# Homes of mLSTM row tiles, y operands and last-stage pools moved; loads and splits at three seams issued in order of use

## The chip, the core and the metric

The kernel runs on one core of one Trainium2 chip. The metric is device time in microseconds (us) of one execution; the figure for a kernel is the median of its runs. The changed kernel computes the same function with the same matrix products.

## The reference, cut to what matters

```python
# layer 0: mLSTM mixer (x: 2048 tokens x 1024), layer 1: RG-LRU mixer, then a final RMSNorm
u = rmsnorm(x, ln_g[0])
xm, z, o_pre, i_pre, f_pre = split(u @ w_in)                # 2048 wide each, gates 4 heads
xc = silu(causal_dwconv(xm, conv_w, conv_b))
q, k, v = xc @ w_q * DK**-0.5, xc @ w_k, xm @ w_v           # per head
h = mlstm_chunkwise(q, k, v, log_i, log_f)                  # C_new = d*C + sum w k v ; num/den
y = (norm(sigmoid(o_pre) * h) * norm_w + skip * xc) * silu(z)
x = x + y @ w_out
u = rmsnorm(x, ln_g[1])
xr, g = split(u @ r_w_in)                                   # 1536 wide each
xc = causal_dwconv(xr, ...)
r, ig = sigmoid(xc @ w_a + b_a), sigmoid(xc @ w_x + b_x)    # 8 diagonal blocks of 192
hs = linear_scan(exp(log_a), sqrt(-expm1(2*log_a)) * ig * xc)
x = x + (hs * silu(g)) @ r_w_out
out = rmsnorm(x, final_g)
```

## The kernel before, in words

Activations lie transposed, 128 channels by 512 (or 256) tokens. Every fp32 product is done as three fp32r matmuls: `split_into` makes a high part (`hi`, a cast on ScalarE, line 790) and a low part (`lo`, a subtraction on VectorE, line 793), and `mm3` (lines 390 to 392) multiplies hi by hi, and hi and lo crosswise. Weights come as fp32 (`raw`) and are split on the spot, or come back already split from a store in DRAM (`kept`). Names with `d_` are arrays in DRAM.

There are four stages.

- **a1**: the input projection, by a Strassen-like scheme of seven products of half-sized blocks, run by a `Slab` object. It stores xm, xc, z, o and the decay rows to DRAM.
- **a2**: the mLSTM, 4 heads by 8 blocks of 256 tokens. A block loads its `xm`, `xc`, `sz`, `o`, and two row tiles broadcast over the partitions, `qb` and `db` (function `rows`). GpSimd masks `qb`, ScalarE makes the weights `wgt` from it, VectorE multiplies the projected q by `db` (`qd`); then come k (`kT`, line 950), the scores (`s`, line 965), v from `vwh`/`vwl`, the state `C` and its split `Ch`/`Cl`, numerator `n`, and the result `hh` (line 1057), which is normalised (`frs`, on GpSimd) and stored as `d_y`.
- **b1**: the out-projection with the residual. `x1_slab(s)` runs once for each half of the tokens, again by seven products in the order u11, t2, u21, t3, t1, t4, u22. Its operands are quarters of y (`y_load`, quarters 11, 12, 21, 22, four tiles `t` each), or sums and differences of them (`into`, line 1225). `get_y` splits an operand ahead of its use, `stream` loads and splits a weight ahead of its use; both run at high priority. Behind them come the RMS sums (`ssum`, line 1142, and `stx`, line 1145, called by `stat`) and the input projection of layer 1 (`early`, `alternate`, groups), which stores `xr` and the gate `g`.
- **b2**: the gates of the RG-LRU (`gate`, from 768 KB weights `wg`), the scan, and the last projection (`acc`, from 512 KB weights `wr`). A block of 512 tokens has four parts p = 0 to 3 of three tiles each; a part's gates use two `wg` tiles, 18 matmuls each. `xch`/`xcl` are the split operand of a part, `yh`/`yl` the split result of one.

Each engine, and each DMA queue (SP's and GpSimd's), takes its instructions strictly in the order in which they were put. That order is made by a scheduler from the program's order, its priorities, and `order(first, then)`, which makes `then` follow `first` on the same engine. Tiles come from pools; a tile's place in SBUF is shared in time with earlier tiles, and the first write to it waits until the earlier tile's last reader is done.

In the kernel before, `y_load` puts all loads of y behind the last instruction of the last block's normalisation: `self.order(self.rooted, (d,))` (line 1213).

The pools of b2 are opened, on the left side of SBUF, in the order r4, y4, w4, x4, g4, t4 (`w4` holds `wr`, `g4` holds `wg`, `t4` holds `xc`, `x4` holds `xch`/`xcl`, `y4` holds `yh`/`yl`).

Of the kernel before, what the change touches and what calls it, by code (L numbers as in the profile page):

```python
# [14 lines left out]
P = 128  # L15
# [33 lines left out]
class Slab:  # L49


    def __init__(self, K, ctx, gain, paired=False, banks=None):
# [22 lines left out]
        self.places = {}  # L75
# [10 lines left out]
    def pair(self, nm, j, dtype=F32):  # L86

        return (self.ta if nm in ("t3", "u22") else self.tp).tile([P, 2 * TB], dtype, tag=f"{nm}{j}", name=f"{nm}{j}")
# [27 lines left out]
    def split(self, t, keep=None):  # L116

        w = t.shape[1]
        both = self.slot(w)
        hi, lo = both[:, 0:w], both[:, w:2 * w]  # L120
        self.K.split_into(hi, lo, t, "a", "v")
        if keep is not None:
            self.nc.gpsimd.dma_start(keep, both.bitcast(F32))
        return hi, lo
# [213 lines left out]
class Trunk:  # L338
# [465 lines left out]
    def phase_a2(self, wq, wk, wv, rgate, rwout, D, late):  # L804
# [3 lines left out]
        with ExitStack() as ctx:  # L808
# [69 lines left out]
            def project(h, b):  # L878
# [7 lines left out]
                def rows():  # L886
                    S["qb"] = qb = lp.tile([P, 2, P], F32, tag="qb", name="qb")
                    S["db"] = db = lp.tile([P, BL], F32, tag="db", name="db")
                    nc.sync.dma_start(qb, D["q"][r0:r0 + 2].rearrange("c t -> (c t)").partition_broadcast(P)
# [3 lines left out]
                def loads():  # L893
# [6 lines left out]
                    nc.sync.dma_start(xc, D["xc"][hs, :, bs].rearrange("k p t -> p k t"))  # L900
                    nc.sync.dma_start(xm, D["xm"][hs, :, bs].rearrange("k p t -> p k t"))
# [5 lines left out]
                    nc.sync.dma_start(sz, D["sz"][hs, :, bs].rearrange("k p t -> p k t"))  # L907
                    self.loaded = (nc.sync.dma_start(o, D["o"][b * 2:b * 2 + 2, :, h * DV:(h + 1) * DV].rearrange("c p n -> p c n")),)
                    for nm, x in (("xc", xc), ("xm", xm)):
# [9 lines left out]
                def qk():  # L919
# [3 lines left out]
                    wgt = dp.tile([P, 2, P], F32, tag="wgt", name="wgt")  # L923
                    for c in range(2):
                        a = nc.scalar.activation(wgt[:, c], qb[:, c], AF.Exp, bias=self.gT[:, r0 + c:r0 + c + 1],
                                                 scale=-1.0)
                        if (h, b) == (0, 1):
                            self.order((self.kT,), (a,))
                    S["wgt"] = wgt
                    xh, xl = S["xc"]  # L930
                    for nm in ("q", "k"):
# [6 lines left out]
                        t = dp.tile([P, 2, BL], F32, tag=nm + "T", name=nm + "T")  # L938
# [17 lines left out]
                    for k in range(KV):  # L956
                        nc.scalar.activation(skx[:, k], S["xcf"][:, k], AF.Copy, scale=self.v("sk", h * KV + k))
# [44 lines left out]
            def recur(h, b, c, S):  # L1002
# [12 lines left out]
                def update(m):  # L1015
# [14 lines left out]
                    self.split_into(Ch, Cl, Cm, "a", "v")  # L1030
# [24 lines left out]
                else:  # L1055
                    hh = dp.tile([P, DV], F32, tag="hh", name="hh", bufs=3)
                nc.vector.scalar_tensor_tensor(hh.rearrange("p (a b) -> p a b", a=2), pn[:, :, 0:256], da[:, 1:2],
                                               S["o"][:, c].rearrange("p (a b) -> p a b", a=2),
                                               op0=ALU.mult, op1=ALU.mult)
# [102 lines left out]
    def phase_b1(self, xT, wout, rwin, D, outT, banks, lates):  # L1162
# [3 lines left out]
        with ExitStack() as ctx:  # L1166
# [17 lines left out]
            def stream(n=2):  # L1184
                with tc.high_priority():
                    while order and len(ready) < n + (order[0][0] == "early"):
# [3 lines left out]
                        else:  # L1190
                            ready.append(S.weights(rwin[i], D["wr"][i], s, None if kind == "s" else kind))
                return ready.pop(0)

            def w_weights(nm, k):
# [3 lines left out]
                nc.sync.dma_start(r, wout[k + 8 * (nm[1] == "2"), :, 512 * (nm[0] == "2"):512 * (nm[0] == "2") + 512])  # L1198
                return S.split(r)

            homes = ({"12": "t4", "11": "t3", "21": "t2", "22": "t1"}, {"11": "t4", "22": "t3", "12": "t2", "21": "t1"})
            X = {}

            def y_load(s, q, eng, js=range(4)):
# [3 lines left out]
                for j in js:  # L1208
# [4 lines left out]
                    self.order(self.rooted, (d,))  # L1213
# [4 lines left out]
            def get_y():  # L1218
                with tc.high_priority():
                    while ahead and len(ys) < 3:  # L1220
# [6 lines left out]
                        def chain(v):  # L1227
                            self.order(led, (v,))
                            led[:] = [v]
# [10 lines left out]
                        a, v = self.split_into(hi, lo, src, "a", "v")  # L1240
                        if (s, nm, k) == (0, "u11", 3):
# [6 lines left out]
                return ys.pop(0)  # L1248
# [105 lines left out]
            def g_out(m2, s):  # L1354
                def out(mi, ni, put):
# [4 lines left out]
                    def rest():  # L1360
                        if s == 1 and m2 == NG - 1:
                            t = wk("gt")[:, 0:TB]
                            nc.scalar.activation(t, g, AF.Tanh, scale=0.5)
# [449 lines left out]
```

## Time and profile before

| what | value |
|---|---|
| median of 3 runs | 2929.7 us (2927.17 to 2930.38) |
| profiled execution | 2925.95 us |
| its span in the trace | 2923.9 us |
| TensorE clock granted, mean | 0.991 |
| TensorE busy | 2820.2 us, 96% |
| VectorE / ScalarE / GpSimd busy | 73% / 52% / 15% |
| DMA | 687.36 MB, mean 235 GB/s |

The span is the time from the first to the last instruction of the profiled execution; the rest of its time lies around the span. TensorE is the busiest engine, and what it isn't busy is spread over few places. Each instruction of the trace has a start, a duration, and, where its engine was idle before it, the length of that idle time and what ended it (`[7.24 <-DMA wg<-d_gw]`). `SPq` is the queue of DMA issues of SyncE.

### The profile page before, as it was taken

How to read it: one execution, taken by the hardware profiler on the slowest of the kernel's cores; microseconds unless marked ns; L12 is line 12 of the kernel's file. 1: busy time of each engine (PE TensorE's matmuls, PEld its weight loads, DVE VectorE, ACT ScalarE, POOL GpSimd, SP SyncE). 2: the span in 40 equal slices, each digit the busy share in tenths (PEclk: the TensorE clock that was granted, in tenths of full speed). 3: DMA queues.
4: the chain of work that ended last, by engine and by line, in shares of the span. 5: the costliest groups of instructions: out<-in, count | busy, mean ns of one | idle time of the engine just before them, and what ended most of it. 6: DMA issues, size and time to landing. Idle time of an engine off the chain costs nothing. (4 is left out here: it accounts for less than half of the span.)

```text
span 2923.9 us, 43286 instructions
## 1 busy us (share of the span) xinstructions
PE 2820.2 (96%) x15442; PEld 2436.8 (83%) x15442; DVE 2126.1 (73%) x3594; ACT 1516.8 (52%) x2547; POOL 447.7 (15%) x846
## 2 busy tenths in 40 slices
PE   7999999999999899999999989999999999899998
PEld 5799987889987799898989868888788888678886
DVE  7766789535568488888888866768889657766764
ACT  6444556424345466666667543435434323876761
POOL 1211122101123111111111111101221111000000
PEclk9999999999999999999999999999999999999999
DMA  6766677668899745556676478876776665788865
GB/s 229 266 224 226 248 245 272 196 202 291 276 322 300 253 151 184 172 194 193 189 228 194 134 256 276 296 236 215 244 251 227 232 202 184 281 309 304 286 214 201
DMA packets 295543, 687.36 MB, mean 235 GB/s; under 512 B 29088, under 2 KB 107680, under 8 KB 295328
## 3 DMA queue, kind: packets, MB, share of 16 engines
q1 hardware_dynamic: 228144, 451.13, 48.2%
q0 software_dynamic: 66608, 232.43, 21.2%
q8 instruction: 121, 1.98, 0.3%
q10 hardware_dynamic: 576, 1.05, 0.1%
q14 instruction: 94, 0.77, 0.1%
HBM read 447.32 MB, written 237.17 MB: 234 GB/s over the span
## 5 line engine op out<-in xcount | busy, mean ns | idle before, releaser
L790 ACT CAST s<-raw 128x512 fp32r<-128x512 f32 (+1 forms) x280 | 172.7, 620 | 249.2 <-PE pd L392 69.8
L793 DVE TENSOR_TENSOR s<-raw,s 128x512 fp32r<-128x512 f32 (+1 forms) x280 | 191.7, 688 | 53.4 <-ACT s L790 52.3
L390 PE MATMUL acc<-yh,wr 128*128 128x512 f32 x384 | 148.7, 392 | 4.9 <-ACT yh L790 3.3
L391 PE MATMUL acc<-yl,wr 128*128 128x512 f32 x384 | 149.5, 389 | 1.1 <-DVE yl L793 1.1
L392 PE MATMUL acc<-yh,wr 128*128 128x512 f32 x384 | 149.5, 389 | 0.0
L790 ACT CAST u<-t 128x512 fp32r<-128x512 f32 x112 | 69.1, 620 | 147.5 <-PE pc L392 48.0
L717 DVE SCALAR_TENSOR_TENSOR xc<-xm,vec,xc 128x512 f32<-128x512 f32 x192 | 139.2, 746 | 6.2 <-ACT xc L715 5.5
L793 DVE TENSOR_TENSOR u<-t,u 128x512 fp32r<-128x512 f32 x112 | 76.7, 689 | 73.9 <-ACT u L790 73.7
L790 ACT CAST s<-sum 128x512 fp32r<-128x512 f32 (+1 forms) x120 | 74.0, 618 | 108.6 <-PE pc L392 44.3
L391 PE MATMUL pa<-u,s 128*128 128x512 f32 x304 | 119.7, 394 | 7.3 <-DVE u L793 7.3
L392 PE MATMUL pa<-u,s 128*128 128x512 f32 x304 | 119.5, 393 | 0.0
L790 ACT CAST Ch<-C 128x516 fp32r<-128x516 f32 x120 | 74.8, 623 | 86.2 <-DVE da L1047 57.4
L390 PE MATMUL pa<-u,s 128*128 128x512 f32 x304 | 118.5, 396 | 0.0
L1027 DVE SCALAR_TENSOR_TENSOR C<-C,dl,kv 128x516 f32<-128x516 f32 x112 | 83.5, 745 | 47.0 <-PE kv L392 47.0
L717 DVE SCALAR_TENSOR_TENSOR xc<-xr,vec,xc 128x512 f32<-128x512 f32 x144 | 106.1, 748 | 9.7 <-ACT xc L715 8.4
L390 PE MATMUL pj<-vwh,xmh 128*128 128x512 f32 x256 | 103.0, 404 | 3.9 <-ACT vwh L790 3.8
L391 PE MATMUL pj<-vwl,xmh 128*128 128x512 f32 x256 | 100.3, 392 | 1.8 <-DVE vwl L793 1.8
L392 PE MATMUL pj<-vwh,xml 128*128 128x512 f32 x256 | 99.9, 390 | 0.0
L793 DVE TENSOR_TENSOR s<-sum,s 128x512 fp32r<-128x512 f32 (+1 forms) x120 | 82.5, 689 | 21.7 <-ACT s L790 20.8
L390 PEld LDWEIGHTS acc<-yh,wr 128*128 128x128 f32 x384 | 71.8, 188 | 22.8 <-ACT yh L790 5.0
L390 PE MATMUL pd<-u,s 128*128 128x512 f32 x224 | 87.4, 390 | 0.0
L793 DVE TENSOR_TENSOR Cl<-C,Ch 128x516 fp32r<-128x516 f32 x120 | 82.8, 690 | 6.1 <-ACT Ch L790 5.7
(499 smaller groups left out, 10014.3 us busy)
## 6 DMA issues: line engine op xcount, KB each, us to landing
wr<-d_ow SPq DMA_DIRECT2D x96, 512.0 KB, 4.7
d_wx<-s POOLq DMA_DIRECT2D x64, 512.0 KB, 4.5
s<-d_wx SPq DMA_DIRECT2D x64, 512.0 KB, 4.3
s<-d_ws SPq DMA_DIRECT2D x64, 512.0 KB, 6.1
raw<-in_wxz_dram SPq DMA_DIRECT2D x124, 256.0 KB, 4.7
d_wr<-s POOLq DMA_DIRECT2D x48, 512.0 KB, 3.5
s<-d_wr SPq DMA_DIRECT2D x48, 512.0 KB, 4.5
raw<-in_rwin_dram SPq DMA_DIRECT2D x94, 256.0 KB, 4.0
```

Of the source, the lines that this page charges most:

```text
L390: mm(out, sh, mh, start=first, stop=False, skip_group_check=resumed)
L391: mm(out, sh, ml, start=False, stop=False, skip_group_check=resumed)
L392: mm(out, sl, mh, start=False, stop=last, skip_group_check=resumed)
L717: nc.vector.scalar_tensor_tensor(out, x[:, j:j + TB], self.v(wn, m * 4 + j), out, op0=ALU.mult, op1=ALU.add)
L790: a = nc.scalar.copy(hi, src)
L793: b = (nc.gpsimd if lo_eng == "p" else nc.vector).tensor_tensor(lo, src, hi.bitcast(F32), op=ALU.subtract)
L1027: nc.vector.scalar_tensor_tensor(C2, C2, self.dl[:, r:r + 1], p2, op0=ALU.mult, op1=ALU.add)
```

## The change

Four groups of edits.

1. **a1 to a2.** `qb`, `db`, `wgt`, `qT` and `kT` move from the pools `lp` and `dp` to the pool `lx`, so their places are others. For the first block the loads of `qb` and `db` come right after its `xc` and `xm`, ahead of the loads of the v weights, `wgt` comes right after the last `z` activation, and the loads of block (0, 2) wait for those of block (0, 0). `skx` of all later blocks comes after the cast `Ch`.
2. **a2 to b1.** The places of t1 and t4 move to the pool `ta`, ahead of the raw weights. Loads of y's quarters 22 and 12 of the first half no longer follow `rooted`. The loads of quarter 11 and of the first eight raw weights alternate on SP, and their splits follow one chain on VectorE with those of the y operands; `hh` comes ahead of the first u splits. Two rounds of `get_y` and `prefetch` come before `x1_slab`.
3. **`stat`** runs at high priority.
4. **b1 to b2.** The pools of b2 are opened in the order r4, x4, y4, t4, g4, w4. The split of part p = 2's operand comes before the last tanh and multiplication of `g`, and that of p = 3 after the split of part 0's result.

```diff
-        return (self.ta if nm in ("t3", "u22") else self.tp).tile(...)
+        return (self.ta if nm in ("t3", "u22", "t1", "t4") else self.tp).tile(...)
...
-                    S["qb"] = qb = lp.tile([P, 2, P], F32, tag="qb", name="qb")
-                    S["db"] = db = lp.tile([P, BL], F32, tag="db", name="db")
+                    S["qb"] = qb = lx.tile([P, 2, P], F32, tag="qb", name="qb")
+                    S["db"] = db = lx.tile([P, BL], F32, tag="db", name="db")
...
+                    if (h, b) == (0, 2):
+                        self.order(self.begun, first + (S["rows"],))
...
+                        if (h, b) == (0, 0):
+                            self.order(self.tail[-1:], (a,))
...
+                        if (h, b) != (0, 0):
+                            self.order(self.state[:1], (a,))
...
-                    self.order(self.rooted, (d,))
+                    if s or q not in ("22", "12"):
+                        self.order(self.rooted, (d,))
+                    if (s, q) == (0, "11"):
+                        X11.append(d)
...
+                        if (s, nm) == (0, "u11") and k < 3:
+                            self.order(self.state[:1], (a,))
+                            self.order((self.scaled,), (v,))
...
+            for n in (1, 2):
+                get_y(n)
+                prefetch(n)
...
-                    for b in (2, 3):
-                        rcs[b] = S.invrms(saccs[b])
+                    with tc.high_priority():
+                        for b in (2, 3):
+                            rcs[b] = S.invrms(saccs[b])
...
+                if b == 0 and p == 3:
+                    self.order(self.ysplit, cast)
                 if b == 0 and p == 2:
-                    self.order(cast, self.ysplit)
+                    self.order(cast, self.ysplit + self.tanh + (self.gated,))
...
             rp = ctx.enter_context(tc.tile_pool(name="r4", bufs=2, reuse_waits="tile"))
+            xp = ctx.enter_context(tc.tile_pool(name="x4", bufs=2, reuse_waits="tile"))
             yp = ctx.enter_context(tc.tile_pool(name="y4", bufs=4, reuse_waits="tile"))
+            tp = ctx.enter_context(tc.tile_pool(name="t4", bufs=2, reuse_waits="tile"))
+            gp = ctx.enter_context(tc.tile_pool(name="g4", bufs=3, reuse_waits="tile"))
             wp = ctx.enter_context(tc.tile_pool(name="w4", bufs=4, reuse_waits="tile"))
-            xp = ctx.enter_context(tc.tile_pool(name="x4", bufs=2, reuse_waits="tile"))
-            gp = ctx.enter_context(tc.tile_pool(name="g4", bufs=3, reuse_waits="tile"))
-            tp = ctx.enter_context(tc.tile_pool(name="t4", bufs=2, reuse_waits="tile"))
```

What this does to the order of instructions is seen at three places. At the seam from a1 to a2, SP's queue before, from the first block's `xc` (`qb_10001` and `db_10002` are the first block's rows, `wraw` the v weights):

```order
L900 DMA xc_9998<-d_xc_82 128x4x256
L901 DMA xm_9997<-d_xm_81 128x4x256
L840 DMA wraw_10083<-in_wv_dram 128x4x256
L840 DMA wraw_10089<-in_wv_dram 128x4x256
L900 DMA xc_10155<-d_xc_82 128x4x256
L901 DMA xm_10154<-d_xm_81 128x4x256
L901 DMA xm_10405<-d_xm_81 128x4x256
L889 DMA qb_10001<-d_q_88 128x256
L891 DMA db_10002<-d_dec_89 128x256
```

and now:

```order
L900 DMA xc_9998<-d_xc_82 128x4x256
L901 DMA xm_9997<-d_xm_81 128x4x256
L889 DMA qb_10001<-d_q_88 128x256
L891 DMA db_10002<-d_dec_89 128x256
L840 DMA wraw_10083<-in_wv_dram 128x4x256
L840 DMA wraw_10089<-in_wv_dram 128x4x256
L889 DMA qb_10150<-d_q_88 128x256
L891 DMA db_10151<-d_dec_89 128x256
L900 DMA xc_10155<-d_xc_82 128x4x256
```

The two row loads moved past five larger loads, two of which wait for VectorE.

At the seam from a2 to b1, GpSimd's queue before (the `frs` rows are the last block's normalisation; `t_18876` and the seven after it are quarters 22 and 12 of the first half of y, `t_18975` and on are quarter 21):

```order
L1097 DMA d_y<-y 128x4x256
L1070 TENSOR_SCALAR frs<-mv 128x2
L1072 TENSOR_SCALAR frs<-mv 128x2
L1071 TENSOR_TENSOR frs<-frs,mh 128x2
L1073 TENSOR_TENSOR frs<-frs 128x2
L1211 DMA t_18876<-d_y 128x2x512
L1211 DMA t_18878<-d_y 128x2x512
L1211 DMA t_18880<-d_y 128x2x512
```

and now:

```order
L1236 DMA t_18888<-d_y 128x2x512
L1236 DMA t_18890<-d_y 128x2x512
L1107 DMA d_y<-y 128x4x256
L1080 TENSOR_SCALAR frs<-mv 128x2
L1082 TENSOR_SCALAR frs<-mv 128x2
L1081 TENSOR_TENSOR frs<-frs,mh 128x2
L1083 TENSOR_TENSOR frs<-frs 128x2
L1236 DMA t_18975<-d_y 128x2x512
```

All eight loads (the last two are shown) now stand ahead of the last store of y and of the last normalisation.

At the seam from b1 to b2, SP's queue before (`wg_25560` and `wg_25562` are the two weights of part p = 1's gates, `wg_25594` the first of p = 2; `xc_25542`, `xc_25551`, `xc_25637` the operands of p = 1, 2, 3):

```order
L1459 DMA wg_25560<-d_gw_94 128x1536
L1459 DMA wg_25562<-d_gw_94 128x1536
L1544 DMA g_25544<-d_g_87 128x3x512
L1544 DMA g_25607<-d_g_87 128x3x512
L1502 DMA xc_25542<-d_xr_86 128x3x512
L1502 DMA xc_25551<-d_xr_86 128x3x512
L1459 DMA wg_25594<-d_gw_94 128x1536
L1459 DMA wg_25646<-d_gw_94 128x1536
L1459 DMA wg_25753<-d_gw_94 128x1536
```

and now:

```order
L1538 DMA xc_25542<-d_xr_86 128x3x512
L1538 DMA xc_25551<-d_xr_86 128x3x512
L1538 DMA xc_25637<-d_xr_86 128x3x512
L1582 DMA g_25544<-d_g_87 128x3x512
L1582 DMA g_25607<-d_g_87 128x3x512
L1495 DMA wg_25560<-d_gw_94 128x1536
L1495 DMA wg_25562<-d_gw_94 128x1536
L1495 DMA wg_25594<-d_gw_94 128x1536
L1495 DMA wr_25648<-d_ow_95 128x1024
```

The operands moved ahead of all gate weights. On VectorE, at the same seam, before (`gt_25514` is the last tanh of b1, in b1's pool of work tiles):

```order
L302 TENSOR_TENSOR g_25512<-pd_25461,u2_25343 128x512
L1364 TENSOR_SCALAR gt_25514<-gt_25514 128x512
L1605 TENSOR_TENSOR g_25544<-xc_25301,g_25544 128x1536
L1365 TENSOR_TENSOR g_25512<-g_25512,gt_25514 128x512
L793 TENSOR_TENSOR xcl_25553<-xc_25551,xch_25552 128x1536
```

and now:

```order
L302 TENSOR_TENSOR g_25512<-pd_25461,u2_25343 128x512
L793 TENSOR_TENSOR xcl_25553<-xc_25551,xch_25552 128x1536
L1396 TENSOR_SCALAR gt_25514<-gt_25514 128x512
L1643 TENSOR_TENSOR g_25544<-xc_25301,g_25544 128x1536
L1397 TENSOR_TENSOR g_25512<-g_25512,gt_25514 128x512
```

The split of part 2's operand moved ahead of the last multiplication of `g`. By the pools' new order, the place of `wg_25562` overlaps that of `gt_25514`, so its load now waits for the multiplication at the end of this piece; the places of `yh` of part 0 overlap those from which part 1's gates read their operand.

More of the change, by code (lines that the diff above doesn't have):

```diff
@@ L74, in __init__ @@
         self.rx, self.rxs = self.rg, ExitStack()
-        self.places = {}
+        self.places, self.made = {}, ()
     def open(self):
@@ L1197, in w_weights @@
                 r = S.raw()
-                nc.sync.dma_start(r, wout[k + 8 * (nm[1] == "2"), :, 512 * (nm[0] == "2"):512 * (nm[0] == "2") + 512])
-                return S.split(r)
+                d = nc.sync.dma_start(r, wout[k + 8 * (nm[1] == "2"), :, 512 * (nm[0] == "2"):512 * (nm[0] == "2") + 512])
+                both = S.split(r)
+                if nm == "11" and len(begun) < 8:
+                    begun.append(d)
+                    chain(S.made[1])
+                    if k == 0:
+                        self.order(X11[0:2], (d,))
+                    if k in (2, 4):
+                        self.order((d,), X11[k // 2 + 1:k // 2 + 2])
+                    if k in (3, 5):
+                        self.order(X11[k // 2 + 1:k // 2 + 2], (d,))
+                return both
             homes = ({"12": "t4", "11": "t3", "21": "t2", "22": "t1"}, {"11": "t4", "22": "t3", "12": "t2", "21": "t1"})
-            X = {}
+            X, X11 = {}, []
             def y_load(s, q, eng, js=range(4)):
@@ L1212, in y_load, with chain, get_y @@
                                       D["y"][k:k + 2, :, bs].rearrange("k p n -> p k n"))
-                    self.order(self.rooted, (d,))
+                    if s or q not in ("22", "12"):
+                        self.order(self.rooted, (d,))
+                    if (s, q) == (0, "11"):
+                        X11.append(d)
             ahead = [(s, nm, k) for s in range(2) for nm, _ in steps for k in range(8)]
             ys, led = [], []
-            def get_y():
+            def chain(v):
+                self.order(led, (v,))
+                led[:] = [v]
+            def get_y(n=3):
                 with tc.high_priority():
-                    while ahead and len(ys) < 3:
+                    while ahead and len(ys) < n:
                         s, nm, k = ahead.pop(0)
@@ L1362, in rest @@
                             t = wk("gt")[:, 0:TB]
[L1363 to L1364 removed]
+                            self.tanh = (nc.scalar.activation(t, g, AF.Tanh, scale=0.5),
+                                         nc.vector.tensor_scalar(t, t, 0.5, 0.5, op0=ALU.mult, op1=ALU.add))
                             nc.vector.tensor_tensor(g, g, t, op=ALU.mult)
@@ L1609, in gates @@
                 if early:
-                    self.cast, self.ysplit = a[:1], a
+                    self.cast, self.ysplit, self.gated = a[:1], a, gated
+                    self.order(a[:1], (carry,))
                 ys += [(hi[:, to], lo[:, to]) for to in range(3)]
```

45 lines of the change are left out of this document (24 added, 21 removed).

## The prediction

> **What bounds the kernel now.** I read the busy times first, then the waits of TensorE over the whole span, then the time lines of the engines at each place where a wait stands. Here are TensorE's busy line and its waits (waited for, us in total, times, longest):
>
> ```profile
> PE 2820.2 (96%) x15442; PEld 2436.8 (83%) x15442; DVE 2126.1 (73%) x3594; ACT 1516.8 (52%) x2547; POOL 447.7 (15%) x846
> ...
> PE s L965 <- ACT kT L950: 8.9, 4, 6.0
> PE pa L391 <- DVE u L793: 7.3, 1, 7.3
> PE gate L390 <- DMA wg<-d_gw: 7.2, 1, 7.2
> ...
> PE n L390 <- DVE hh L1057: 4.2, 4, 2.5
> ...
> PE pb L390 <- DVE stx L1145: 2.8, 1, 2.8
> ...
> PE pd L391 <- DVE t L793: 2.6, 1, 2.6
> ...
> PE gate L390 <- ACT xch L790: 1.7, 1, 1.7
> ```
>
> TensorE bounds the span: a us is gained only where it stands still or runs cold. These waits add up to 35 us, and most of it lies at the three seams and in one stretch of b1. The change takes away no matmul, so its worth is what it takes from these waits, and from the slow matmuls behind them, less what it adds.
>
> **Seam 1, a1 to a2.** The first scores wait for `kT`. The chain, from the time lines of SP, GpSimd, VectorE, ScalarE and TensorE (start, duration, engine, line, operation, [idle before]):
>
> ```profile
> 995.52 1.71 SPq L840 DMA_DIRECT2D wraw<-in_wv_dram  x2
> 1000.66 0.78 SPq L889 DMA_DIRECT2D qb<-d_q  x1
> 1008.62 0.42 POOL L921 TENSOR_SCALAR_AFFINE_SELECT qb<-qb 128x256 f32<-128x256 f32 x1 [7.47 <-DMA qb<-d_q]
> 1010.08 0.69 DVE L942 SCALAR_TENSOR_TENSOR qd<-pj,db 128x512 f32<-128x512 f32 x1 [9.85 <-DMA db<-d_dec]
> 1011.33 0.58 ACT L950 COPY kT<-pj 128x512 f32<-128x512 f32 x1
> 1005.65 0.28 PE L392 MATMUL pj<-xch,kwl 128*128 128x256 f32 x1
> 1011.96 2.08 PE L965 MATMUL s<-qT,kT 128*128 128x128 f32 x8 [6.03 <-ACT kT L950]
> ```
>
> `kT` itself needs only the k product, whose last matmul starts at 1005.65; it comes 5.4 us later because ScalarE works in order and stands before it for `wgt` and `qh`, which need the two row loads. These are issued at 1000.66 and later, behind the v weights and others, and `qb` arrives 8 us after its issue. Moved up to before 995.52, the loads land by about 1003 even with that same 8 us, which is when the q product is done; `kT` then follows the k product: 1005.93 + 0.58 = 1006.5, and `s` starts at 1006.6 in place of 1011.96. The v product behind it keeps its distance, since `vwh` and `vwl` are next on ScalarE and VectorE and move with `kT`; the v weights, put behind two 128 KB rows, land well before 1006. Gain 5.4. The `skx` now behind `Ch` is read only at the end of a block, ScalarE being 52% busy: 0. Lower end 3.5, if the v weights come 2 us late; upper end 5.9, all of the 6.03 but the issue.
>
> **Seam 2, a2 to b1.** The loads of y, then TensorE around them:
>
> ```profile
> 1697.67 0.84 POOL L1097 DMA_DIRECT2D d_y<-y  x1 [15.12 <-ACT s L790]
> ...
> 1704.75 5.83 POOL L1211 DMA_DIRECT2D t<-d_y  x8 [0.30 <-issue]
> 1714.53 1.23 DVE L1225 TENSOR_TENSOR t<-t,t 128x1024 f32<-128x1024 f32 x1 [11.13 <-DMA t<-d_y]
> ...
> 1692.17 0.36 PE L390 MATMUL n<-vh,sh 128*128 128x258 f32 x1 [2.53 <-DVE hh L1057]
> ...
> 1694.43 0.39 PE L390 MATMUL pa<-u,s 128*128 128x512 f32 x1
> 1694.66 0.39 PE L391 MATMUL pa<-u,s 128*128 128x512 f32 x1
> ...
> 1716.42 0.80 PE L391 MATMUL pa<-u,s 128*128 128x512 f32 x1 [7.28 <-DVE u L793]
> ...
> 1729.12 2.08 PE L390 MATMUL pb<-u,s 128*128 128x512 f32 x4 [2.44 <-ACT u L790]
> ...
> 1732.58 0.40 PE L391 MATMUL pb<-u,s 128*128 128x512 f32 x1
> ```
>
> Matmuls start 0.23 apart here (1694.43, 1694.66; 0.2275 over a longer run). Product u11 is 8 operands x 4 banks x 3 = 96 of them, 21.8 us; it begins at 1694.43, so without a stop the next, t2, would begin at 1716.3. It begins at 1729.12, and its first 8 matmuls take 3.46 (to 1732.58) in place of 1.82. The seam thus loses 12.8 + 1.6 = 14.5 us, of which the two named waits are only 9.7; the rest are matmuls at half speed behind them.
>
> The cause is VectorE, which stands in line 1225 for y loads that GpSimd issues only at 1704.75, behind `frs`; the u split that u11 needs is queued behind that subtraction. In the changed order these eight issues (5.83 / 8 = 0.73 each) stand ahead of the last store of y and its `frs`, on places whose last readers are TensorE's products of the last block, done by 1684; they go out between 1683 and 1690, and with the 9.8 us that the first took (1704.75 to 1714.53) the first pair is there at 1693, before VectorE asks. The price: the last `d_y` store and the `frs` behind it wait for those eight issues, up to 6 us of GpSimd, which the trace covers, since `d_y` goes out at 1697.67 and the issues end by 1690. Then VectorE has the subtractions (1.23 each) between the splits of u11, 4.9 us in a product of 21.8 us whose 16 splits of weights and operands take 11: it fits, tightly in the first half, where the last `hh` stands too. I take 13.7 of the 14.5. Putting `hh` ahead of two u splits (0.6 us each) gives back 1.3 of the 2.53. Together 15.0; ends 10.5 (VectorE's 4.9 us come on the path) and 16.5.
>
> **The stretch behind x1.** The busy time of the engines in three stretches (window, its length, PE, PEld, DVE, ACT, POOL, granted clock, DMA share, GB/s), and the time lines of VectorE and TensorE in the first:
>
> ```profile
> 2020.00:2075.00 55.00, 49.63 (x222) 40.42 (x222) 50.74 (x84) 31.43 (x55) 12.20 (x20) 0.97 0.70 232
> 2495.00:2585.00 90.00, 78.49 (x330) 62.13 (x330) 66.78 (x52) 71.32 (x88) 1.62 (x3) 0.96 0.78 279
> 1700.00:1730.00 30.00, 20.28 (x75) 15.88 (x74) 12.11 (x18) 6.48 (x11) 10.68 (x16) 0.81 1.00 380
> ...
> 2069.53 0.15 DVE L1145 TENSOR_SCALAR stx<-ssum 128x4 f32<-128x4 f32 x1
> ...
> 2064.23 0.50 PE L391 MATMUL pd<-t,s 128*128 128x512 f32 x1 [2.57 <-DVE t L793]
> ...
> 2066.64 0.39 PE L392 MATMUL pd<-t,s 128*128 128x512 f32 x1
> 2069.83 0.47 PE L390 MATMUL pb<-t,s 128*128 128x512 f32 x1 [2.80 <-DVE stx L1145]
> ...
> 2073.78 0.40 PE L390 MATMUL pc<-t,s 128*128 128x512 f32 x1
> ```
>
> `stx` reads the sums that hold two PSUM banks. At high priority it moves up on VectorE by 60 to 70 instructions, which at 0.6 apart are some 40 us; the banks come free, and TensorE has the products `pb` and `pc` to run while it now waits for `t`. Lost here: 2.57, 2.96 (2066.87 to 2069.83), and ten matmuls in 3.95 us in place of 2.28: 7.2 in all. VectorE stays full (50.7 of the 55 us from 2020 to 2075), so what it owes TensorE doesn't vanish: I leave 2.0 and take 5.2; ends 2.0 (only the bank wait goes, and half of that returns) and 6.5.
>
> On the cold matmuls: behind the 2.44 us wait the next ones start 0.43 apart, behind the 2.57 us wait they start 0.23 apart at once. The Trainium skill, "TensorE: Matmul & The Clock Gate", Part 1, says that the clock is halved after an idle window of about 3.4 us that runs freely; by that rule the 1 us stops left here would bring no cold matmuls, and the sum stands as it is; by the row at 1729.12, where a stop shorter than the window did bring them, it would be 1.6 smaller.
>
> **Seam 3, b1 to b2.** SP, TensorE, VectorE, and the loads of gate weights (KB each, median us to landing):
>
> ```profile
> 2506.91 0.36 SPq L1502 DMA_DIRECT2D xc<-d_xr  x1
> 2507.32 1.56 SPq L1459 DMA_DIRECT2D wg<-d_gw  x3
> ...
> 2498.45 0.39 PE L390 MATMUL gate<-raw,wg 128*128 128x512 f32 x1
> 2506.38 0.39 PE L392 MATMUL gate<-raw,wg 128*128 128x512 f32 x1
> 2514.01 1.19 PE L390 MATMUL gate<-xch,wg 128*128 128x512 f32 x2 [7.24 <-DMA wg<-d_gw]
> ...
> 2506.09 0.43 DVE L1364 TENSOR_SCALAR gt<-gt 128x512 f32<-128x512 f32 x1 [1.05 <-ACT gt L1363]
> 2508.10 0.69 DVE L1365 TENSOR_TENSOR g<-g,gt 128x512 f32<-128x512 f32 x1
> ...
> wg<-d_gw SPq DMA_DIRECT2D x30, 768.0 KB, 5.5
> ```
>
> Before, part 1's 36 matmuls run from 2498.45 to 2506.6, and then TensorE waits for part 2's weight, since SP stood until 2506.91 at the load of part 2's operand. This operand now comes early. But the second weight of part 1, which was there in time before, now waits for the multiplication that ends at 2508.79, and that one comes 1.76 us of split later, less the 1.05 that VectorE was idle: issue at about 2509.4. With 5.0 us to land (a little under the 5.5, as less is on the way) TensorE goes on at 2514.4, with 18 matmuls more to do than before: 18 x 0.2266 = 4.1. So it is 4.5 late there. The wait for `xch` (1.7) goes. What replaces it: `yh` of part 0 lies on the operands of part 1, so ScalarE can't cast it until TensorE is through part 1 at about 2518.6, 5 us after the 2513 of before, and the rates of part 1 follow it; ScalarE is busy 71 of the 90 us from 2495 to 2585, so of these 5 us I let 1.2 arrive at TensorE. Loss 4.5 − 1.7 + 1.2 = 4.0; ends 0 (the later small waits for `yh`, `yl` go as well) and 8.5 (all of ScalarE's delay arrives). On the 5.0: the Trainium skill, "DMA: Bandwidth & Descriptors", Anatomy of one DMA, gives a fixed 2.0 us and the bytes over 436 GB/s, here 3.8 us by estimate; the sum would be 1.2 better by it, but no row here shows a gate weight arriving so fast, the median being 5.5.
>
> **The sum.** −5.4 − 15.0 − 5.2 + 4.0 = −21.6. The profiled execution, 2925.95, becomes 2904.3; it lies 3.75 under the median of the runs, 2929.7, so the median becomes 2908.1. The ends add to −28.9 and −7.5: 2900.8 and 2922.2.
>
> **Rivals.** (A) *Seam 3 is the new bound.* The gate weight's wait and ScalarE's late `yh` both arrive in full, and behind `yh` the scan of part 1 and `acc`: 4.5 + 7 = 11.5 in place of 4.0. For it speaks that ScalarE is the second busiest there; against it that two waits of before go. Time 2908.1 + 7.5 = 2915.6. (B) *Seam 2 gives half.* The y loads, moved over the loads of quarter 11 and of the raw weights, share the DMA engines with them, and u11 waits for its own weights instead; twelve tiles of y (0.52 MB each) and eight raw weights (0.26), 8.4 MB, take 22 us at the 380 GB/s of the busiest 30 us. Against it: they are needed over the 22 us of u11, beginning 10 us after the first issue. Gain 7.5: 2915.6. (C) *All gains, no price at seam 3*, the weight landing in 3 us and ScalarE's slack taking the rest: 2904. (D) *Slower*: at seam 3 SP stands at the gate weight with every later load behind it. If the last tanh, now behind the split of part 2's operand, waits for that operand's load, then the tanh, the multiplication, the weight and TensorE all wait in turn. Each us that the load lands after 2504 is a us lost; with 25.6 gained elsewhere and 4.0 lost already, it decides for slower by over 0.2% from 2504 + 27.5 on. Against it: the load stands ahead of all gate weights, and one of its size takes 5.5. (E) *The change doesn't do what it says*: `qb` or y loads still go out late since their new places are not free; then −5.2 and +4.0 alone remain, about 2928.
>
> **How the numbers follow.** Forecast 0.56, A 0.14, B 0.11, C 0.11, D 0.03, E 0.05. The time is the forecast's, 2908. The range reaches from the lower end, 2900, past A and B to the upper end, 2922, and leaves out D, E and the tails. A measurement of this kernel tells about 0.2%, 5.9 us, from no change. Faster by more than that: the forecast, A, B and C, less their tails, 0.90; within: most of E and some of A and B together, 0.06; slower: D and the rest, 0.04.
>
> **What would show it.** Right: the first `s` near 1006.6 with no wait for `kT` over 1 us; all eight y issues before 1692, no wait of `pa` for `u` over 1, t2 beginning near 1709 in its span (1729.12 less 15.0 and 5.4); `stx` within 10 us of `ssum`; at seam 3 one wait of `gate` for `wg` of 9 to 12 us, in the middle of part 1. Wrong: VectorE's subtractions standing in front of u splits, a wait of `gate` or `acc` for ScalarE of over 3, or cold clocks at a place that is warm now.

## The result, and the profile after

| | before, same chip | after | ratio (95% interval) |
|---|---|---|---|
| median | 2930.04 us (6 runs, 2927.17 to 2934.56) | 2914.25 us (6 runs, 2911.81 to 2917.18) | 0.9946 (0.9933 to 0.9958) |
| the same again, on another chip | 2932.53 us (9 runs) | 2913.04 us (`ctrl`, below) | 0.9939 (0.9926 to 0.9951) |

The change makes the kernel 15.8 us faster, 19.5 in the repeat; forecast were 21.6. The time lies in the range given, 6 us over the forecast of 2908.1. The profiled execution of after took 2917.18 us, the slowest of its six, while that of before, 2925.95, is faster than any of the runs here. So the places below are read from the repeat's profile too (span 2911.3 us), and only what both show is called an effect.

TensorE's busy line of after, and its waits over the span (us in total, times, longest):

```profile
PE 2829.2 (97%) x15442; PEld 2439.3 (84%) x15442; DVE 2125.0 (73%) x3594; ACT 1516.9 (52%) x2547; POOL 448.0 (15%) x846
...
PE gate L390 <- DMA wg<-d_gw: 8.6, 2, 4.9
PE kv L390 <- DVE C L1035: 8.3, 24, 2.1
...
PE s L973 <- ACT kT L956: 3.7, 4, 1.7
...
PE acc L390 <- ACT yh L790: 3.0, 4, 0.8
...
PE pa L390 <- ACT y L1103: 1.5, 1, 1.5
...
PE n L390 <- DVE hh L1065: 1.3, 3, 0.5
```

Of the waits that the prediction listed, those for `u`, `stx`, `t` and `xch` are gone, `kT` fell from 8.9 to 3.7 and `hh` from 4.2 to 1.3. The wait for `wg` rose from one of 7.2 to two with 8.6. One number fits no wait: TensorE is busy 9.0 us longer (2820.2 before), with the same 15442 matmuls.

Where the time came from and went, by the start of the same matmul in two traces (negative: earlier than before, in us):

| place (time before) | forecast | after | change there | repeat | change there |
|---|---|---|---|---|---|
| a1 to 990 | 0 | +3.1 | +3.1 | +1.3 | +1.3 |
| seam 1, to 1020 | −5.4 | −2.5 | **−5.6** | −4.3 | **−5.6** |
| first block of a2, to 1040 | 0 | +3.2 | **+5.7** | +1.8 | **+6.1** |
| to 1640 | 0 | +6.0 | +2.8 | +2.3 | +0.5 |
| late a2, to 1660 | 0 | +2.0 | **−4.0** | −1.7 | **−4.0** |
| seam 2, to 2020 | −15.0 | −12.4 | **−14.4** | −16.1 | **−14.4** |
| behind x1, to 2440 | −5.2 | −18.3 | **−5.9** | −22.0 | **−5.9** |
| seam 3, to 2590 | +4.0 | −14.8 | **+3.5** | −18.7 | **+3.3** |
| rest of b2, to 2915 | 0 | −8.5 | **+6.3** | −12.6 | **+6.1** |

a1 and the stretch to 1640 differ between the two profiles of one kernel, so nothing is built on them. The other rows repeat within 0.4 us. Four were forecast, three were not: the loss in the first block, the gain late in a2, and the loss in the rest of b2, where after has no wait that before had not.

The forecast places, in lines of after's time lines (start, duration, engine, line, operation, [idle before]); the first three lines are seam 1, the next three seam 2, the last two the stretch behind x1:

```profile
996.08 0.33 SPq L889 DMA_DIRECT2D qb<-d_q  x1
1009.08 0.59 ACT L956 COPY kT<-pj 128x512 f32<-128x512 f32 x1 [0.74 <-PE pj L392]
1009.72 1.16 PE L973 MATMUL s<-qT,kT 128*128 128x128 f32 x8 [0.68 <-ACT kT L956]
...
1685.16 0.79 POOL L1236 DMA_DIRECT2D t<-d_y  x1 [0.58 <-issue]
1687.68 5.04 POOL L1236 DMA_DIRECT2D t<-d_y  x7 [1.72 <-issue]
1696.33 0.50 PE L390 MATMUL pa<-u,s 128*128 128x512 f32 x1 [1.51 <-ACT y L1103]
...
2016.95 0.95 PE L1152 MATMUL ssum<-ones,sacc 128*128 128x1 f32 x8
2018.54 0.15 DVE L1155 TENSOR_SCALAR stx<-ssum 128x4 f32<-128x4 f32 x1
```

`qb` is issued ahead of the v weights and `s` follows `kT` at once. The y loads go out between 1685 and 1693. `stx` stands 1.6 us behind `ssum`, where it had stood some 38 us behind. The three stretches that the prediction showed, as they are now (window, its length, PE, PEld, DVE, ACT, POOL, granted clock, DMA share, GB/s):

```profile
2020.00:2075.00 55.00, 53.48 (x233) 42.85 (x232) 49.65 (x83) 33.38 (x58) 11.51 (x22) 1.00 0.82 271
2495.00:2585.00 90.00, 86.92 (x360) 68.90 (x361) 62.24 (x44) 70.13 (x86) 0.00 (x0) 0.97 0.88 313
1700.00:1730.00 30.00, 30.00 (x134) 24.86 (x133) 23.81 (x34) 13.04 (x25) 6.40 (x9) 1.00 1.01 388
```

Seam 2 is full (TensorE is busy 30.00 of 30 us, 20.28 before), and the clock is granted in full.

### The profile page after: what moved, and what is told of

Same layout as the page of the kernel before. It is cut to its first block, busy times and chain, and to the rows that moved or that the text cites. A ratio compares the mean times of both kernels' runs of the same rounds, so it can differ in the third digit from the quotient of the medians.

```text
span 2915.4 us, 43311 instructions
## 1 busy us (share of the span) xinstructions
PE 2829.2 (97%) x15442; PEld 2439.3 (84%) x15442; DVE 2125.0 (73%) x3594; ACT 1516.9 (52%) x2547; POOL 448.0 (15%) x846
## 5 line engine op out<-in xcount | busy, mean ns | idle before, releaser
L390 PE MATMUL pd<-u,s 128*128 128x512 f32 x224 | 87.1, 389 | 0.0
L391 PE MATMUL pd<-u,s 128*128 128x512 f32 x224 | 87.1, 389 | 0.0
```

The lines of the kernel that those rows point to most:

```text
L390: mm(out, sh, mh, start=first, stop=False, skip_group_check=resumed)
L391: mm(out, sh, ml, start=False, stop=False, skip_group_check=resumed)
```

## The experiments

All are timed in five rounds beside the kernel before on their chip (2932.53, 2930.63 and 2931.44 us in the three batches). Where a text says how far TensorE is ahead or behind, it compares the start of the same matmul in two traces, one profile of each kernel. Diffs are against after unless they say otherwise.

### `ctrl`, `align`, `rows`, `seam3`: where the losses are

`ctrl` is after unchanged.

> The changed kernel as it is, a second profile of it. If the late losses seen in the first profile (block 0 of a2: 5.4 us; first block of head 1: 3.2 us; matmul spacing of 232 ns in place of 227 ns in b2: 5.8 us over b2; 3.1 us in a1) are the kernel's, they are there again; those that are chance are not. Time: 0.9946 of before, 2914 us, within 3 us.

Measured: 2913.04 us, ratio 0.9939. Two of the late losses are there again, those of the first block of a2 and of b2; that of the first block of head 1 is not, and that of a1 is 1.3 in place of 3.1.

```diff
 align
             tp = ctx.enter_context(tc.tile_pool(name="t4", bufs=2, reuse_waits="tile"))
+            pd = ctx.enter_context(tc.tile_pool(name="pad4", bufs=1, reuse_waits="tile"))
+            pd.tile([P, 96], F32, tag="pad", name="pad")
             gp = ctx.enter_context(tc.tile_pool(name="g4", bufs=3, reuse_waits="tile"))
```

> Only a pad of 384 bytes ahead of the pools g4 and w4, so that the gate and output weights start at 352 modulo 512 bytes, as all weights of b1 do, in place of 480. Theory (the start of the stationary operand within 512 bytes sets the spacing of the matmuls): spacing in b2 falls from 232.5 to 227 ns, and the kernel is 5.5 us faster than the control, ends 4 and 7. Rival 1 (the spacing comes from where in SBUF the weights lie, above 165 KB, or from the distance to the other operand): 384 bytes change nothing, within 1.5 us of the control. Rival 2 (it is chance of one run): the control shows 227 ns too.

Measured: 2906.71 us, 0.9916 (0.9902 to 0.9929): 6.3 us less than `ctrl`, by 384 bytes that nothing reads. Here is one whole block of 512 tokens in b2, from one named wait to the same wait a block later (TensorE's time lines of before, after and `align`):

```profile
2670.32 0.97 PE L390 MATMUL acc<-yh,wr 128*128 128x512 f32 x3 [1.18 <-ACT yh L790]
2771.67 0.50 PE L390 MATMUL acc<-yh,wr 128*128 128x512 f32 x1 [1.18 <-ACT yh L790]
```

```profile
2657.18 0.50 PE L390 MATMUL acc<-yh,wr 128*128 128x512 f32 x1 [0.81 <-ACT yh L790]
2760.71 0.50 PE L390 MATMUL acc<-yh,wr 128*128 128x512 f32 x1 [0.81 <-ACT yh L790]
```

```profile
2650.66 0.72 PE L390 MATMUL acc<-yh,wr 128*128 128x512 f32 x2 [1.18 <-ACT yh L790]
2752.02 0.50 PE L390 MATMUL acc<-yh,wr 128*128 128x512 f32 x1 [1.18 <-ACT yh L790]
```

A block takes 101.35 us before, 103.53 after (with a wait that is even 0.37 shorter), and 101.36 in `align`. No engine is waited for: each of the 128x512 matmuls follows the last at 232.7 ns in place of 227.0 (means of 1230 and 1260 distances between starts, after and before, from 2600 to 2900 us; 227.0 in `align`). What differs is where the stationary operands lie: the tiles of `wg` and `wr` start 352 bytes above a multiple of 512 in before and `align`, 480 above one in after. The pool `t4`, now opened ahead of theirs, isn't a multiple of 512 in size. The pad of `align` moves these two pools alone: the moving operands (`xch`, `yh` and their low parts) stay where they are.

```diff
 rows
-                    S["qb"] = qb = lx.tile([P, 2, P], F32, tag="qb", name="qb")
+                    S["qb"] = qb = lx.tile([P, 2, P], F32, tag="qb", name="qb", bufs=3)
...
-                        self.order(self.begun, first + (S["rows"],))
+                        self.order(self.begun, first)
```

`db` has the third buffer too, and both row loads of block (0, 2) are issued right behind those of (0, 1).

> The row loads qb and db of block (0,2) are issued right behind those of block (0,1), into a third buffer, ahead of the larger loads. Theory (ScalarE stands in order at wgt of block (0,2), 5.6 us, because its qb arrives late, and so gives back the gain of seam 1): that wait goes, block 0 of a2 gives back under 1 us in place of 5.4, and the kernel is 4.5 us faster than the control, ends 3 and 5.5. Rival (the DMA engines are full from 995 to 1020, so another load becomes the late one, xm, xc, sz or o of blocks 1 and 2): within 1.5 us of the control.

Measured: 2907.46 us, 0.9917 (0.9905 to 0.993). The place that it mends, in the time lines of after (SP's issues of xm, sz and qb, GpSimd's mask of `qb` and ScalarE's `wgt` of block (0, 2)):

```profile
1004.37 3.06 SPq L901 DMA_DIRECT2D xm<-d_xm  x1
1007.48 2.70 SPq L909 DMA_DIRECT2D sz<-d_sz  x1
1012.90 0.38 SPq L889 DMA_DIRECT2D qb<-d_q  x1
1021.62 0.41 POOL L925 TENSOR_SCALAR_AFFINE_SELECT qb<-qb 128x256 f32<-128x256 f32 x1 [11.65 <-DMA qb<-d_q]
1022.06 0.69 ACT L929 ACTIVATE wgt<-qb,gT 128x128 f32<-128x128 f32 x2 [5.58 <-POOL qb L925]
```

ScalarE, which works in order, stands 5.58 us for a row that was issued at 1012.90 and is there 8.7 us later; the casts of the state behind it are late, and TensorE waits for `C` and `da`. In `rows` this stand is gone, and the first block loses 0.8 us (−3.9 to −3.1) in place of 5.7 to 6.1. So the late row is what costs the gain. Why it is late is another question, and its place on the queue alone is not the answer. In the kernel before, the same row goes out later, but it lands sooner:

```profile
1014.58 0.38 SPq L889 DMA_DIRECT2D qb<-d_q  x1
1019.21 0.41 POOL L921 TENSOR_SCALAR_AFFINE_SELECT qb<-qb 128x256 f32<-128x256 f32 x1 [4.83 <-DMA qb<-d_q]
```

That is 4.6 us from issue to mask (4.7 in `u1`, below), against 8.7 in after (9.1 in `ctrl`). The DMA engines' share from 1014 to 1024 is 0.83 before and 0.87 in `u1`, 0.99 in after and 0.92 in `ctrl`: group 1 has moved larger loads to this time (the two `xm` behind that of block (0, 0) went out by 1000.6 before, and go out at 1004.37 and 1015.49 in after). That the fuller engines alone make the difference was not tried.

In its one profile (2913.02 us, the slowest of its five) the lead of `rows` over `ctrl` then melts in the later heads and is gone at the end; the timed median is 5.6 us better. How much of the 5 us reaches the end is therefore known from the times alone.

```diff
 seam3
-                            sacc = tp.tile([P, TB], F32, tag="sacc", name="sacc")
+                            sacc = qp.tile([P, TB], F32, tag="sacc", name="sacc")
...
             wp = ctx.enter_context(tc.tile_pool(name="w4", bufs=4, reuse_waits="tile"))
+            qp = ctx.enter_context(tc.tile_pool(name="q4", bufs=2, reuse_waits="tile"))
```

> The small tiles of the last stage (sacc, sq, rb) move behind the weights into a pool of their own; so g4 and w4 lie lower (152416 and 170848), no gate weight overlaps the last gate tile of b1, and both weight pools start at 352 modulo 512. Theory (the two waits of gate for wg, 3.7 and 4.9 us, and the cold matmuls behind them are the price of seam 3, and the weights' start sets the spacing): 4 to 5 us from the waits and 5.5 from the spacing, together 9.5 us faster than the control, ends 7 and 12. Rival (ScalarE's chain of yh and the rates takes the place of the weights): only the spacing, 5.5 us. If the spacing theory is wrong too: 0 to 4.

Measured: 2898.85 us, 0.9888 (0.9873 to 0.9903): 14.2 us less than `ctrl`, more than the upper end expected. The tiles `sq`, `rc`, `rb` and `stx` move likewise. With the statistics' tiles out of `t4`, the pool of `wg` no longer lies over the last gate tile of b1, and its tiles start at 352 again. The longest of TensorE's waits from 2470 to 2590, `seam3`:

```profile
PE acc L390 <- DMA wr<-d_ow: 7.2, 1, 7.2
```

Both waits for `wg` are gone; a new one for `wr` is there, since the loads of `wr` stand on SP behind those of `wg` that wait for matmuls. Even so TensorE is 26.6 us ahead of before at 2590 (`ctrl`: 18.7): 6.8 us come from the seam (`seam3` wins 3.6 there, `ctrl` loses 3.3), where 4 to 5 were expected, and most of the rest from the distance of the matmuls in b2.

### `u1`, `u2`, `u3`, `u4`: one group undone at a time

`u1` takes back all of group 1.

> Seam 1 alone undone: the row tiles and their orders stand as in the kernel before, everything else as after. Theory: the 5.6 us that seam 1 won are given back in the first block of head 0, since the row loads of block (0,2) land late (ScalarE stood 5.58 us at its weights). Then the profile shows the wait of the first score product for k back at about 6 us, the matmuls 5 to 6 us later there than in the repeat of after, but level with it (within 1 us) at the end of head 0; the time within 1.5 us of the repeat (2911.5 to 2915) if the 3.9 us that every variant of after won late in head 3 come from somewhere else, and some 4 us longer (2915 to 2918) if those come from the order of the skip activations, which this kernel also undoes. Rival, the prediction's own sum: seam 1's gain of 5.4 us reaches the end, and the time is 2917 to 2920 with the matmuls late by 5 us from seam 1 on to the end of the second stage without a change between.

Measured: 2920.82 us, 0.9966 (0.9955 to 0.9977), 6.6 to 7.8 more than after, over all that was expected. Its trace says why. At the first scores it is 5.6 us behind `ctrl`; at 1040 the two are level within 0.3 us, so seam 1's gain was indeed given back in one block. It then wins 0.8 us late in a2 where after wins 4.0, and 4.0 us less at seam 2 (10.4 in place of 14.4), where TensorE waits three times for ScalarE's splits (1.16, 0.78, 0.61). The late gain has its cause in the time lines of before:

```profile
1637.05 0.91 ACT L957 ACTIVATE skx<-xc,vec 128x256 f32<-128x256 f32 x2 [6.03 <-DMA xc<-d_xc]
1641.05 0.39 PE L390 MATMUL kv<-vh,kh 128*128 128x258 f32 x1 [2.17 <-ACT vh L994]
```

ScalarE stood 6.03 us at `skx` for a load, with `vh` behind it; after puts `skx` behind the casts of the state, and the wait is gone; in `u1` ScalarE stands at `skx` for 5.24 us again. So group 1 pays late in a2, by its last edit, and at seam 2, not at seam 1. Which of its edits helps seam 2 is open, since all were taken back at once.

`u2` puts one condition back.

```diff
 u2
-                    if s or q not in ("22", "12"):
-                        self.order(self.rooted, (d,))
+                    self.order(self.rooted, (d,))
```

> One condition of seam 2 undone: all loads of y's quarters wait again for the last block's statistics; the early splits and the pair places stay as in after. Theory: the gain at seam 2 (14.4 us in after's profile, 14.5 in the repeat) rests on the loads of quarters 22 and 12 going out ahead, so 9 to 14.5 us are lost: 2922 to 2928. Rival: the gain comes from the splits ordered ahead and the first load's place, and those two quarters are needed late enough to land in time anyway (they are first read by the sums after the first product): a loss under 3 us, 2913 to 2916.

Measured: 2926.58 us, 0.9986 (0.9978 to 0.9995), 12.3 to 13.5 us more than after. The longest of TensorE's waits from 1680 to 1740:

```profile
PE pa L392 <- DVE s L793: 7.8, 1, 7.8
```

The seam gains 2.7 us in place of 14.4, and VectorE stands for y again (10.98 us, 11.13 before). The early issue of these two quarters is most of seam 2's gain; the rest of group 2 brings 2.7 without it.

`u3` takes the high priority from `stat`.

> One edit undone: the sums of the statistics behind x1 are emitted without high priority, as in the kernel before; everything else as after. Theory: the 5.9 us that after's profile won between 2020 and 2185 us come of this edit alone and reach the end: 2917.5 to 2921. Rival: the stretch is shorter because seam 2 brought its operands early, and the order of the statistics is worth under 2 us: 2913 to 2916.

Measured: 2914.66 us, 0.9948 (0.9935 to 0.996): no loss: the time is the rival's, its reason is not. The first of these two fences holds TensorE's waits from 2000 to 2100 in `u3`, the second those from 2430 to 2600:

```profile
PE pb L390 <- DVE stx L1155: 2.8, 1, 2.8
PE pd L391 <- DVE t L793: 2.6, 1, 2.6
```

```profile
PE gate L390 <- DMA wg<-d_gw: 6.1, 2, 3.4
```

The old waits are back, and TensorE is 6.4 us behind `ctrl` from 2185 to 2480. Then it is 0.5 us behind at 2590: seam 3 loses 6 us less. The reason is an accident of places, read from the addresses of the built kernels and the two traces. The loads of b2's weights lie over the work tiles of b1's gates, which rotate through ten places; the order of `stat` shifts the rotation. The last multiplication of a gate and the issues of `wg` behind it, in `ctrl`:

```profile
2486.66 0.69 DVE L1397 TENSOR_TENSOR g<-g,gt 128x512 f32<-128x512 f32 x1
2487.43 0.99 SPq L1495 DMA_DIRECT2D wg<-d_gw  x2
2492.51 0.80 PE L390 MATMUL gate<-raw,wg 128*128 128x512 f32 x1 [5.25 <-DMA wg<-d_gw]
```

and in `u3`:

```profile
2471.51 8.26 SPq L1494 DMA_DIRECT2D wg<-d_gw  x3
2478.15 0.68 DVE L302 TENSOR_TENSOR g<-pd,p 128x512 f32<-128x512 f32 x1
...
2493.02 0.69 DVE L1397 TENSOR_TENSOR g<-g,gt 128x512 f32<-128x512 f32 x1
2504.58 0.47 PE L390 MATMUL gate<-xch,wg 128*128 128x512 f32 x1 [2.74 <-DMA wg<-d_gw]
```

In `ctrl` the second `wg` lies on the very last gate tile and goes out at 2487.43, behind its multiplication. In `u3` it lies on a tile that the addition ending at 2478.83 reads, and all three `wg` are out by 2479.8; no gate weight lies on the last gate tile there. So as the kernel stands the order of `stat` wins 5.9 us in one place and costs 6 in another.

`u4` puts back the pool order of b2 and its three orders.

> Seam 3 undone: the last stage's pools and its orders stand as in the kernel before, everything else as after. Theory: both losses of the last stage go, the waits for wg (4.0 us net) and the wider spacing of its products (232.8 instead of 227.0 ns, 5.8 us), so about 9.8 us less than after: 2902.5 to 2906, with a spacing of 227 ns. Rival, the prediction's own sum: only the waits go, 4.0 us: 2909 to 2911.

Measured: 2903.43 us, 0.9912 (0.9898 to 0.9925), 9.6 to 10.8 us less than after and `ctrl`, so group 4 is a loss of that size. Seam 3 now loses 1.5 us (the waits for `wg` are gone, and one of 9.4 for `yh` stands there instead), and a block again takes 101.35 us:

```profile
2648.99 0.50 PE L390 MATMUL acc<-yh,wr 128*128 128x512 f32 x1 [1.18 <-ACT yh L790]
2750.34 0.50 PE L390 MATMUL acc<-yh,wr 128*128 128x512 f32 x1 [1.18 <-ACT yh L790]
```

### `a1al`, `best`, `best_s7`, `best_r7`: using what was found

```diff
 a1al
-        return self.sl.tile([P, 2 * self.wide], F32R, tag="s", name="s")[:, 0:2 * w]
+        return self.sl.tile([P, 1024 if self.paired else 1152], F32R, tag="s", name="s")[:, 0:2 * w]
```

with a pad of 64 bytes ahead of these slots, and 8 in place of 10 work tiles (`wk`) in a1 to make room.

> After, with the slots of the first stage's stationary operands padded so that 2827 of its some 2880 products read them from a start of 352 bytes above a multiple of 512 (mixed starts before), at the price of 8 instead of 10 work tiles of one pool in that stage. Theory: the start of the stationary operand sets the spacing of the 128x512 products, which falls in that stage from 232.5 to about 229 ns (its moving operands stay as they are); some 2880 times 3 ns is 8 us less: 2903 to 2908. Rival: in this stage the spacing is set by the moving operands or by the weights that are loaded beside, and stays at 232 ns: 2911 to 2916, or a few us more where the two missing work tiles cost waits.

Measured: 2927.29 us, 0.9991 (0.9982 to 1.0), a loss of 13. The distance of a1's 128x512 matmuls fell as the theory says, from 232.2 to 229.2 ns (1160 of them between 530 and 1000 us; 232.3 to 229.2 in 1060 between 30 and 460). But TensorE, 2.6 us ahead of `ctrl` at 697, is 17 behind at 950. The longest of its waits from 520 to 1030:

```profile
PE oa L391 <- ACT p L586: 7.6, 3, 3.8
```

So the start of the stationary operand bears on the distance in another stage too, with other moving operands, and the stage loses more to its stops than that brings. The two missing work tiles are the likely cause of the stops.

`best` joins `seam3`, `rows`, and one order on SP:

```diff
+                if b == 0 and kind == "r" and i < 3:
+                    self.wfirst = getattr(self, "wfirst", ()) + (a,)
+                if b == 0 and kind == "g" and i == 6:
+                    self.order(self.wfirst, (a,))
```

> Three findings together: the statistics' tiles of the last stage in a pool of their own (2898.85 us alone), the first three loads of wr ahead of the seventh load of wg on the queue, and the third row buffer for block (0,2). Theory: the wait of 7.2 us of the first down product for wr goes (minus 4 to 7 us), and the rows' 1 to 5.6 us come on top: 2886 to 2894. Rival: the loads share one full queue of transfers, so that wg is late by what wr gains, and the rows' gain is lost again in later heads: 2896 to 2900.

Measured: 2892.81 us (4 runs, 2892.07 to 2894.18), 0.9874 (0.986 to 0.9887): 20 to 21 us less than after, the fastest of all by the median. The wait for `wr` is 3.0 (7.2 in `seam3`).

Two tries to have a1's starts as well, on top of `best`: `best_s7` with 7 slots for split weights and 10 work tiles, `best_r7` with 9 work tiles and 7 raw tiles.

> The three findings together (2892.81 us) and the first stage's stationary operands on starts of 352 bytes above a multiple of 512, paid for with 7 instead of 8 slots for split weights, the work tiles staying at 10. Theory: the spacing of that stage's 128x512 products falls from 232.2 to 229 ns as it did in the run with padded slots (2000 to 2880 of them: 6 to 9 us), and the loss of 14 us in that run came from the two missing work tiles (TensorE waited 7.6 us for ScalarE's p); with them back the time is 2884 to 2889. Rival: the stage needs all its buffers, and the missing slot costs as much as the spacing wins, or more: 2891 to 2905.

> As the run before it, paid for with 9 instead of 10 work tiles and 7 instead of 8 tiles for raw weights, the slots staying at 8. Theory: the spacing wins 6 to 9 us, and one missing work tile costs less than half of what two cost (14 to 18 us together): 2886 to 2892. Rival: the first missing tile is the one that counts: 2895 to 2905.

Measured: 2895.47 us (2887.05 to 2903.38; ratio 0.988, 0.9864 to 0.9897) and 2908.41 us (0.9929, 0.9915 to 0.9942). The distance is 229.2 ns in both. With a slot less it is even with `best`, and spreads wider; with a work tile and a raw tile less it is 16 us worse, longer than anything expected of it. That the work tiles alone make the loss isn't settled: `best_r7` took away two things.

## Why the prediction was right, and where not

- **Seam 1.** The term is right (5.6, forecast 5.4): with a1's lateness taken off, the first `s` starts at 1006.6 in both profiles, as forecast. That the gain reaches the end is wrong. The step that failed is one that the working left out: it asked when the loads of block (0, 0) land, and not when those of block (0, 2) do once TensorE comes to them 5.6 us sooner. Their row is there 8.7 to 9.1 us after its issue in place of 4.6, and the gain is lost in one block. `rows` issues it ahead of the larger loads, and the loss is gone. `rows` also adds a buffer and takes the rows out of the new order that puts them behind the loads of block (0, 0), so which of the three it needs is open; that order alone doesn't make them late, since the row went out at 1014.58 before, without it, and at 1012.90 in after.
- **`skx` behind `Ch`**, costed at 0, won 4.0 us late in a2: the working asked who reads `skx` later and not what ScalarE did behind it earlier. `u1` loses most of it, with the wait back.
- **Seam 2.** Right: 14.4, forecast 15.0, by the forecast means; `u2` shows the cause. t2 begins at 1718.3 and not near 1709: the 7.4 us that were not kept from seam 1 and a1 make most of the difference, and the rest of the seam's gain arrives in the matmuls behind, to 1750.
- **Behind x1.** Right in its place (5.9, forecast 5.2). Not right as a term of a sum: `u3` shows that it takes seam 3's price with it.
- **Seam 3.** The size is near (3.3 to 3.5, forecast 4.0), but partly by luck, for the picture is half right: two waits of 3.7 and 4.9, not one of 9 to 12. The second is the forecast one, for the last multiplication. The first, for part 1's first gate weight, was not foreseen: the working put the move of the operands ahead of all gate weights at nothing. SP's issues of `wg`, before and after:

```profile
2484.05 0.90 SPq L1459 DMA_DIRECT2D wg<-d_gw  x2
...
2468.89 23.15 SPq L1495 DMA_DIRECT2D wg<-d_gw  x3
```

Before, the first weight went out ahead of the large loads and landed in 5.7 us, and nobody waited for it. In after it goes out at 2468.89 behind three `xc` and two `g`, with the DMA engines' share at 0.94 from 2465 to 2475, and TensorE goes on only at 2483.95. In `seam3` two weights are ahead of the `xc` again, and the wait is gone. The forecast loss by ScalarE's late `yh` hardly came: TensorE's waits for it from 2470 to 2590 are 1.4 in all. The wait for `xch` is gone, as forecast. The 3.8 us that the prediction works out for a gate weight is not reached: of before's 30 none landed in under 4.1. After's matmuls run at half the rate behind both waits:

```profile
2483.95 0.76 PE L390 MATMUL gate<-raw,wg 128*128 128x512 f32 x1 [3.68 <-DMA wg<-d_gw]
2484.52 0.63 PE L391 MATMUL gate<-raw,wg 128*128 128x512 f32 x1
2484.94 0.63 PE L392 MATMUL gate<-raw,wg 128*128 128x512 f32 x1
...
2490.33 0.39 PE L390 MATMUL gate<-raw,wg 128*128 128x512 f32 x1
2490.56 0.40 PE L391 MATMUL gate<-raw,wg 128*128 128x512 f32 x1
...
2491.05 0.99 SPq L1495 DMA_DIRECT2D wg<-d_gw  x2
2496.07 0.80 PE L390 MATMUL gate<-raw,wg 128*128 128x512 f32 x1 [4.88 <-DMA wg<-d_gw]
2496.66 0.63 PE L391 MATMUL gate<-raw,wg 128*128 128x512 f32 x1
```

Behind the first wait they start 0.42 to 0.43 us apart for 6 us, then 0.23. This is one of the prediction's signs of being wrong: the same matmuls ran warm before, and in after the granted clock is 0.67 from 2485 to 2495. The idle window of some 3.4 us of the Trainium skill, "TensorE: Matmul & The Clock Gate", Part 1, agrees with these two waits of 3.68 and 4.88; the one of 2.44 at 1729.12 in before, which the prediction set against it, was shorter and had the same behind it. Behind the one of 2.74 at 2504.58 in `u3` the slow matmuls come too, 1.2 us after it.

- **The pools of b2.** The working asked of a moved pool only whose place it takes, and at nothing costed where its tiles start. That start is worth 5.7 to 6.3 us of the sum, more than seam 3's net loss. With it falls the working's premise that a us is gained only where TensorE stands still or runs cold: in b2 it loses 6 us doing neither.

The four priced places are each right within 0.7 us and give −22.4 to −22.6 in place of −21.6. The unforeseen pieces cancel only in part: +5.7 to +6.1 in the first block, −4.0 in late a2, +6.1 to +6.3 in b2, together +7.8 to +8.4. On the forecast that is −13.2 to −13.8, against −12.6 in the repeat's profile; the timed medians, −15.8 and −19.5, are better than either, since the profiled run of before is a short one. That the sum came out as near as it did is luck: the late gain in a2 paid for most of what the first block lost. None of the rivals came as told: the time of A, 2915.6, is near, but its waits for ScalarE's `yh` are not there.

## What to carry to other kernels

When a change brings the bound engine sooner to the next block, or moves large loads on a queue, price the next loads as steps of their own: read what stands ahead of them, how full the DMA engines are when they go out, and which engine works in order behind their first reader. When pools move, look up two things for each tile on the bound engine's path: the last reader of the place it takes, which a rotation can shift by an edit far away, and the byte at which it starts. And undo the groups one by one: the whole was 16 us faster, and one of its four groups cost 10.

## What the runs showed of the hardware

At a granted clock of 0.98 to 1.00, the distance between 128x512 matmuls in fp32r depends on where the operands start in a partition, modulo 512 bytes (starts by the addresses of the built kernels). With the stationary operand at 352 it is 227.0 ns, at 480 it is 232.7, with the moving operand at 352 both times (b2, `align` against `ctrl`, 6.3 us in the time). Sorted by the start of the stationary operand within before's trace of a1, 352 and 32 give 229.7 to 230.6, and 0, 64, 384, 416, 448 and 480 give 232.2 to 233.5; with all at 352 (`a1al`) the same stage falls to 229.2.

The start of the moving operand has a part too. Sorted by it, the same distances of `a1al` from 530 to 1000 us are 228.2 at 96 (676 of them) and 228.4 at 352 (209), but 232.2 at 480 (155), though the stationary operand is at 352 in all. This is a sorting of one run; no run moves the moving operand alone. Whether the two starts count each by itself or by how they lie to each other, and why 352 is better than 480, stays open.
